# First part of the probabilities' transposes at the beginning of an attention step

## The chip, the cores and the metric

One core of one Trainium2 chip runs the whole program; the weights and activations are in its HBM at the start and the result is written there. The metric is the device time in microseconds (us). Three runs of the kernel before gave 1155.04, 1155.28 and 1155.72 us, median 1155.28. Matrix products and transposes run on TensorE (PE), elementwise work and reductions on VectorE (DVE), activations and copies on ScalarE (ACT), some elementwise work on GpSimd (POOL). SyncE (SP) issues most transfers. Each engine works through its own queue in order and waits there for what it needs from the others.

## The reference

A decoder of two layers on a sequence of 512 tokens with a width of 1024. Layer 1 is a retention layer. Its result gives keys and values once for layer 2, which is a sparse attention: 16 heads in 4 groups, each head with a compressed branch, a branch over selected blocks and a window branch. The change lies in layer 2. For 512 tokens the 8 blocks of 64 all fit into the selection of 16, and the window is 512 long, so the second and third branch are plain causal attentions over all keys, with keys and values of their own:

```
s = einsum('bgrqd,bgkd->bgrqk', q, k) * scale
p = softmax(where(valid, s, NEG), axis=-1)
o = einsum('bgrqk,bgkd->bgrqd', p, v)
out = gates[..., 0:1] * o_c + gates[..., 1:2] * o_s + gates[..., 2:3] * o_w
y = (silu(gate) * out) @ w_out
h = h + y
```

A gated per-layer embedding and an RMS norm end each layer and the network.

## The kernel before

Every matrix product in fp32 is made of three products of rounded parts (`mm3`, line 349: high by high, high by low, low by high). So each operand has a high part, written by an ACT copy, and a low part, written by a DVE subtraction; `split_psum` (line 363) does both from an accumulator bank. All accumulators are PSUM banks of 128 x 512, by tag (line 272): "d" 2 banks for dense work, "s" 3 for scores, "pt" 2 for transposes, "o" 1 for a head's result. A tag's banks are taken in turn, and a bank is taken again when all who read it are done.

The order of the instructions on every engine is the order in which the program issues them; nothing is scheduled anew. Weights come as a stream of blocks of 512 KB: `W.tick(2)` (line 146) issues, twice, the low part of one weight block on DVE (line 205), the high part of another on ACT (line 190) and the gain of a third on POOL (line 176); each low part also lets SP issue the next block's transfer.

Layer 2 is a loop over 4 groups (`g`) of 8 steps (`u`, line 1036). A step belongs to head `u // 2` and branch `u % 2`: branch 0 is the selected one, whose keys also hold the 32 compressed keys, branch 1 the window. In step `u` the kernel does these things, in the order of lines 1045 to 1077:

- `scores` of the next step (line 912): the products of queries and keys into three "s" banks, then on DVE the causal mask (lines 942, 945), the maximum of each row (947) and the compressed scores (951), and on ACT the exponentials with their sums (954). The products have 15 matmuls in odd steps, whose next branch has compressed keys, and 12 in even ones.
- `fill(0)`, `fill(1)`, `fill(2)`: pieces of dense work, each 12 matmuls on PE. They come in a fixed order by `between` (line 34) and `PLAN` (line 1032): halves of a gate projection (evacuated by line 752 on ACT and 753 on DVE), halves of a query projection (739 and 740), pairs of tiles of the output projection of a pair of heads (1015 on DVE, one "d" bank for each tile). A step has one to four of them.
- `scale_probs` of the next step (line 960): the reciprocal of the sums and the gate on DVE (963, 964), then four scalings of the probabilities in place on POOL (967).
- `probs_T(u, 0)` (line 969): two "pt" banks of four transposes of the step's own probabilities (line 976), each followed by its `split_psum` into the operands `tH` and `tL`.
- `probs_T(u, 1)`: the two transposes that are left, into one more bank ("pt", or "d" where no dense piece stands before it), and its split.
- `W.tick(2)`, the rest of the compressed branch's softmax, and in even steps `cmp_T` (line 902): four transposes of the compressed probabilities into a "pt" bank (line 906), which ACT (909) and DVE (910) evacuate.
- `values` (line 981): the products of the transposed probabilities with the values into "o", in odd steps followed by the head's gating and split (993 to 995).

`probs_T` and `values` share the single pair `tH`, `tL`. The probabilities have two buffers. Step 7 of a group projects the next group's keys before anything else; after it the next group's values are projected through "d" and "pt" banks in turn (line 1083), each with a split. In the very first step `fill(0)` stands ahead of the scores.

Of the kernel before, what the change touches and what calls it, by code (L numbers as in the profile page):

```python
# [33 lines left out]
def between(g, h):  # L34

    def out(g, pair):
        return [("nout", g, 2 * pair), ("nout", g, 2 * pair + 1)]

    if g == 3:
        return ([("gate", 3, 0)] + out(2, 1), [("gate", 3, 1), ("gate", 3, 2)], out(3, 0),  # L40
                [("gate", 3, 3), ("emb", 1, 0), ("emb", 1, 1)])[h]
    q = [("q", g + 1, h - 1), ("q", g + 1, h)]
    if g == 0 and h < 2:
        return q if h else [("gate", 0, 0), ("gate", 0, 1)]
    return [("gate", g, h)] + (q if h % 2 else out(g - (h == 0), int(h == 0)))
# [191 lines left out]
def decoder(ctx: ExitStack, tc: tile.TileContext, x, xT, stream, cst, msk, gains, fnorm, out):  # L237
# [34 lines left out]
    def psum(tag, shape=None):  # L272
        n = {"d": 2, "s": 3, "pt": 2, "o": 1}[tag]
        return ps.tile([128, 512], F32, name=tag, bufs=n)
# [88 lines left out]
    def split_psum(h, l, src):  # L363
        act.activation(h, src, AF.Copy)  # L364
        dve.tensor_sub(l, src, h.bitcast(F32))  # L365
# [21 lines left out]
    for k in range(NK):  # L387
        g = gn[:, G_RET + k:G_RET + k + 1]
# [85 lines left out]
    def run(g):  # L474
        for _ in g:
            pass
# [235 lines left out]
    def v_proj(g, t, p, bank="d", tick=True, o=None):  # L712
        if o is None:
            o = psum(bank)[:, :256]
            v_sums(t, o, p, 0)
        else:
            v_sums(t, o, p[2:], 6)
        split_psum(v2H[:, t], v2L[:, t], o[:, :256])
        if g == 0:
            act.activation(bg[:, t], o[:, 256:], AF.Tanh, scale=0.5)  # L720
        if tick:
            W.tick()
        if t == 3:
            for q in p:
                q.done()

    def v_pieces(g):
        if g == 0:
            return [W.get("kvb", r, min(384, 1024 - r), 0, 304) for r in (0, 384, 768)]
        return [W.get("kvv", 512 * a, 512, 256 * g, 256) for a in (0, 1)]  # L730
# [27 lines left out]
    def k_proj(g, b):  # L758
        p = W.get("kv", 0, 1024, 1024 + 512 * b + 128 * g, 128)
        o = psum("d")  # L760
        wst(p, o)
        if b == 0:
            m = slice(32 * g, 32 * g + 32)
            pool.tensor_copy(k2H[0][:, :32], kcH[:, m].bitcast(F32))
            pool.tensor_copy(k2L[0][:, :32], kcL[:, m].bitcast(F32))
        e = 0 if b else 32
        split_psum(k2H[b][:, e:], k2L[b][:, e:], o)
        W.tick()
        p.done()
# [132 lines left out]
    def cmp_T(h):  # L902

        p = psum("pt")
        for i in range(NT):
            pe.transpose(p[:96, 128 * i:128 * i + 128], pc4[h % 2][:, i].rearrange("p r n -> p (r n)"),
                         ident)
        d = pcat[h % 2]
        act.activation(d[:96], p[:96], AF.Copy)
        dve.tensor_sub(d[64:96], p[64:96], d[64:96].bitcast(F32))  # L910
# [49 lines left out]
    def scale_probs(g, u, sm_):  # L960
        h, b = divmod(u, 2)
        Pu = P[u % 2]
        dve.reciprocal(sm_, sm_)
        dve.tensor_mul(sm_, sm_, bg[:, :, 12 * g + 3 * h + b + 1])
        for i in (3, 2, 0, 1):
            w = Pu[:, PO[i]:PO[i] + 128 * i + 128]
            pool.tensor_scalar(w, w, sm_[:, i:i + 1], 1.0, op0=OP.mult, op1=OP.mult)  # L967

    def probs_T(u, part, tag="pt"):
        Pu = P[u % 2]  # L970
        for j0, bank in (((0, (0,)), (1, (1, 3))), ((2, (2,)),))[part]:
            p = psum(tag)
            f = 0
            for j in bank:
                for i in range(j, NT):
                    pe.transpose(p[:, f:f + 128], Pu[:, PO[i] + 128 * j:PO[i] + 128 * j + 128], ident)  # L976
                    f += 128
            c = slice(TO[j0], TO[j0] + f)
            split_psum(tH[:, c], tL[:, c], p[:, :f])

    def values(g, u, o):
        h, b = divmod(u, 2)
        if b:
            pe.matmul(o, vcat[:96, 128 * g:128 * g + 128], pcat[h % 2][:96], start=False, stop=False)
        for j in (0, 1, 3, 2):
            n = 512 - 128 * j
            c = slice(TO[j], TO[j] + n)
            d = slice(128 * b, 128 * b + 128)
            mm3(o[:, 128 * j:], [(v2H[:, j, d], v2L[:, j, d], tH[:, c], tL[:, c])], u % 2 == j == 0,
                b == 1 and j == 2)  # L990
        if b:
            y = g2[h % 2]
            dve.scalar_tensor_tensor(y, o, 0.5, y, op0=OP.mult, op1=OP.mult)
            act.activation(y2H[:, h % 2], y, AF.Copy)
            dve.tensor_sub(y2L[:, h % 2], y, y2H[:, h % 2].bitcast(F32))
# [21 lines left out]
    def fillers(g):  # L1017
        for kind, *i in (b for h in range(4) for b in between(g, h)):
            yield from {"gate": g_proj, "q": q_proj, "nout": pair_tiles, "emb": emb_tiles}[kind](*i)
# [14 lines left out]
    for g in range(GROUPS):  # L1034
        f = fillers(g)
        for u in range(8):
            h = u // 2
            last = (g, u) == (3, 7)
            W.auto = False
            left = 2 * len(between(g, h))  # L1040
            first = 4 if h == 3 else left // 2
            n = PLAN[u] if g == 3 else left - first if u % 2 else first
            steps = [1, 1, 0] if last else PARTS[n]

            def fill(i):
                for _ in range(steps[i]):
                    next(f)

            sums = None
            if u < 7:  # L1050
                nxt = g, u + 1
            elif g < 3:
                k_proj(g + 1, 0)
                k_proj(g + 1, 1)
                nxt = g + 1, 0
            else:
                nxt = None
            if g == u == 0:
                fill(0)
            if nxt:  # L1060
                sums, chain = scores(*nxt)
            if g or u:
                fill(0)
            if sums is not None:
                scale_probs(*nxt, sums)
            probs_T(u, 0)
            next(chain, 0)
            fill(1)
            probs_T(u, 1, "pt" if steps[1] else "d")
            W.tick(0 if last else 2)  # L1070
            next(chain, 0)
            if u % 2 == 0:
                cmp_T(h)
            fill(2)
            if u % 2 == 0:
                o_head = psum("o")
            values(g, u, o_head)
            W.auto = True
        run(f)
        if g < 3:  # L1080
            p = v_pieces(g + 1)
            for t in range(NT):
                v_proj(g + 1, t, p, ("d", "pt")[t % 2], t % 2)
# [101 lines left out]
```

## Time and profile before

The profiled execution took 1155.31 us; its span on the core, from the first instruction's start to the last one's end, is 1153.3 us.

| what | value |
|---|---|
| median of 3 runs | 1155.28 us |
| profiled execution, its span | 1155.31 us, 1153.3 us |
| PE busy | 1132.1 us (98%) |
| DVE busy | 710.4 us (62%) |
| ACT busy | 486.7 us (42%) |
| POOL busy | 317.4 us (28%) |
| loop over the steps | 597.7 to 1081 us |

A row of a timeline gives the start of one instruction or of several merged ones, the time from the first one's start to the last one's end, the engine, the line, what is written and read, and how many were merged (x12). In brackets stands how long the engine sat idle before it, and what ended that. A wait for several things is put down to the one that came last by the profile. Matmuls are pipelined, so on PE the time from one row's start to the next row's start says what a row costs.

### The profile page before, as it was taken

The numbers are of one execution on the slowest core, as the hardware profiler recorded it, in microseconds if no ns is written. First come the engines' busy times: TensorE is split into PE (matmuls) and PEld (weight loads), VectorE is DVE, ScalarE is ACT, GpSimd is POOL, SyncE is SP. The second block draws the span as 40 slices with busy tenths as digits, with TensorE's granted clock in tenths as the row PEclk, the third lists the DMA queues.
The fourth block names the chain that finished last, engine by engine and source line by source line (L and its number), as shares of the span: only waits on it lengthen the run. The fifth ranks groups of instructions, "written<-read, shape, count | busy, mean of one in ns | idle before, by whom it ended". The sixth has DMA issues, their size and how long they took to land. (4 is left out here: it accounts for less than half of the span.)

```text
span 1153.3 us, 15259 instructions
## 1 busy us (share of the span) xinstructions
PE 1132.1 (98%) x5812; PEld 964.3 (84%) x5812; DVE 710.4 (62%) x1226; ACT 486.7 (42%) x916; POOL 317.4 (28%) x357
## 2 busy tenths in 40 slices
PE   9999999999999999999899999999999999999997
PEld 7888888888888888988777889888898888988886
DVE  4746435544634665656577865778468774788555
ACT  6433223223323454545455433444345443444653
POOL 0212003002200212346645332354153431421012
PEclk9999999999999999999999999999999999999999
DMA  8422331222232123244531211222031211221211
GB/s 329 149 97 73 110 101 55 92 101 74 86 116 73 55 78 106 73 152 160 163 110 56 74 37 39 78 85 66 27 93 55 74 56 44 85 85 44 74 37 73
DMA packets 29593, 101.90 MB, mean 88 GB/s; under 512 B 3536, under 2 KB 3792, under 8 KB 29520
## 3 DMA queue, kind: packets, MB, share of 16 engines
q1 hardware_dynamic: 29088, 100.15, 26.8%
q8 instruction: 45, 0.74, 0.3%
q10 hardware_dynamic: 432, 0.79, 0.2%
q14 instruction: 28, 0.23, 0.1%
HBM read 98.83 MB, written 2.10 MB: 88 GB/s over the span
## 5 line engine op out<-in xcount | busy, mean ns | idle before, releaser
L355 PE MATMUL d<-arenaR 128*128 128x512 f32 (+2 forms) x2904 | 676.5, 386 | 2.4 <-ACT arenaR L136 1.0
L355 PEld LDWEIGHTS d<-arenaR 128*128 128x128 f32 x2904 | 524.5, 188 | 103.2 <-DVE arenaF L753 1.4
L355 PE MATMUL s<-arenaR 128*128 128x512 f32 (+8 forms) x1182 | 239.8, 354 | 0.7 <-ACT arenaR L364 0.5
L205 DVE TENSOR_TENSOR arenaR<-arenaF,arenaR 128x1024 fp32r<-128x1024 f32 (+1 forms) x142 | 191.7, 1369 | 70.5 <-ACT arenaR L190 70.3
L355 PEld LDWEIGHTS s<-arenaR 128*128 128x128 f32 x1182 | 200.3, 188 | 30.6 <-ACT arenaR L364 0.7
L190 ACT ACTIVATE arenaR<-arenaF 128x1024 fp32r<-128x1024 f32 (+1 forms) x142 | 145.8, 1048 | 105.6 <-PE s L355 68.4
L176 POOL TENSOR_TENSOR arenaF<-arenaF 128x512 f32<-128x512 f32 x108 | 135.3, 1276 | 99.2 <-DMA arenaF<-stream_dram 94.7
L355 PE MATMUL o<-arenaR 128*128 128x512 f32 (+3 forms) x744 | 128.8, 322 | 6.3 <-DVE arenaR L792 4.1
L967 POOL TENSOR_SCALAR arenaF<-arenaF 128x512 f32<-128x512 f32 (+3 forms) x128 | 67.2, 545 | 232.3 <-ACT arenaR L364 118.8
L355 PEld LDWEIGHTS o<-arenaR 128*128 128x128 f32 x744 | 114.3, 189 | 19.6 <-DVE arenaR L792 5.1
L954 ACT ACTIVATE arenaF<-s,arenaF 128x512 f32<-128x512 f32 (+3 forms) x128 | 67.1, 526 | 101.4 <-DVE arenaF L947 90.6
L365 DVE TENSOR_TENSOR arenaR<-pt,arenaR 128x512 fp32r<-128x512 f32 (+1 forms) x141 | 82.9, 618 | 36.9 <-ACT arenaR L364 34.3
L364 ACT ACTIVATE arenaR<-pt 128x512 fp32r<-128x512 f32 (+1 forms) x141 | 70.8, 541 | 73.3 <-PE pt L976 35.2
L371 POOL TENSOR_TENSOR arenaF<-arenaF 128x1 f32<-128x1 f32 (+1 forms) x25 | 14.2, 570 | 295.3 <-DVE arenaF L370 295.3
L355 PE MATMUL pt<-arenaR 128*128 128x512 f32 (+1 forms) x384 | 75.9, 349 | 0.0
L355 PEld LDWEIGHTS pt<-arenaR 128*128 128x128 f32 x384 | 62.7, 188 | 9.4
L209 DVE SCALAR_TENSOR_TENSOR arenaR<-arenaF,arenaR 128x512 fp32r<-128x512 f32 x64 | 45.7, 763 | 35.1 <-PE pt L355 21.4
L194 ACT ACTIVATE arenaR<-arenaF 128x512 fp32r<-128x512 f32 x64 | 43.1, 720 | 46.7 <-issue 22.3
L947 DVE TENSOR_REDUCE arenaF<-s 128x1 f32<-128x512 f32 (+3 forms) x128 | 59.9, 489 | 3.3
L1015 DVE TENSOR_TENSOR arenaF<-arenaF,d 128x512 f32<-128x512 f32 x64 | 42.4, 683 | 8.6 <-PE d L355 7.8
L976 PEld LDWEIGHTS pt<-arenaF 128*128 128x128 f32 x318 | 38.3, 141 | 10.7 <-DVE arenaR L365 3.1
L976 PE MATMUL pt<-arenaF 128*128 128x128 f32 x318 | 45.1, 273 | 1.9 <-DVE arenaR L365 1.9
(126 smaller groups left out, 704.8 us busy)
## 6 DMA issues: line engine op xcount, KB each, us to landing
arenaF<-stream_dram SPq DMA_DIRECT2D x174, 512.0 KB, 3.6
arenaF<-xT_dram SPq DMA_DIRECT2D x8, 256.0 KB, 5.3
arenaF<-x_dram SPq DMA_DIRECT2D x4, 512.0 KB, 8.4
out_dram<-arenaF SPq DMA_DIRECT2D x3, 512.0 KB, 2.6
arenaF<-cst_dram SPq DMA_DIRECT2D x4, 256.0 KB, 3.9
arenaF<-stream_dram ACTq DMA_DIRECT2D x2, 256.0 KB, 4.2
arenaF<-stream_dram SPq DMA_DIRECT2D x2, 256.0 KB, 5.9
arenaF<-cst_dram SPq DMA_DIRECT2D x1, 512.0 KB, 9.5
```

The source lines that it names most:

```text
L176: self.nc.gpsimd.tensor_mul(r3[:, k], r3[:, k], g[:, k, None].to_broadcast([128, m // 2, w]))
L190: self.nc.scalar.activation(hi[:, :m * w], raw, AF.Copy)
L194: self.nc.scalar.activation(hi[:, c], raw[:, c], AF.Copy, scale=g[:, k:k + 1])
L205: self.nc.vector.tensor_sub(lo[:, :m * w], raw, hi[:, :m * w])
L209: self.nc.vector.scalar_tensor_tensor(lo[:, c], raw[:, c], g[:, k:k + 1], hi[:, c], op0=OP.mult, op1=OP.subtract)
L355: pe.matmul(o, a, b, start=start and i == 0, stop=stop and i == n - 1)
L364: act.activation(h, src, AF.Copy)
L365: dve.tensor_sub(l, src, h.bitcast(F32))
L947: dve.reduce_max(mx[:, i:i + 1], o[:, f:f + 128 * i + 128], axis=mybir.AxisListType.X, negate=True)
L954: act.activation(Pu[:, PO[i]:PO[i] + n], o[:, f:f + n], AF.Exp, bias=mx[:, i:i + 1], accum_out=sm_[:, i:i + 1])
L967: pool.tensor_scalar(w, w, sm_[:, i:i + 1], 1.0, op0=OP.mult, op1=OP.mult)
L976: pe.transpose(p[:, f:f + 128], Pu[:, PO[i] + 128 * j:PO[i] + 128 * j + 128], ident)
```

## The change

The first part of a step's own transposes is issued at the beginning of the step, ahead of the next step's scores. Before, it stood behind the first dense piece and the scaling of the next probabilities. In the very first step, too, the first dense piece now comes behind the scores.

```diff
             else:
                 nxt = None
-            if g == u == 0:
-                fill(0)
+            probs_T(u, 0)
             if nxt:
                 sums, chain = scores(*nxt)
-            if g or u:
-                fill(0)
+            fill(0)
             if sums is not None:
                 scale_probs(*nxt, sums)
-            probs_T(u, 0)
             next(chain, 0)
             fill(1)
             probs_T(u, 1, "pt" if steps[1] else "d")
```

## Rows read from the trace of the kernel before

**Rows 1.** Busy time in the loop over the steps; PE, PEld, DVE, ACT, POOL, clock, DMA.

```profile
597.70:1081.00 483.30, 478.94 (x2668) 415.67 (x2668) 342.83 (x705) 217.32 (x499) 170.39 (x216) 1.00 0.20 63
```

**Rows 2.** Waits of PE in the loop: us in total, times, longest.

```profile
PE pt L976 <- DVE arenaR L365: 1.9, 3, 1.1
...
PE d L355 <- DVE arenaF L753: 0.9, 1, 0.9
...
PE pt L906 <- POOL arenaF L967: 0.9, 4, 0.3
```

**Rows 3.** Timeline of PE in step 1.1: start us, us, what.

```profile
736.39 2.49 PE L355 MATMUL s<-arenaR 128*128 128x512 f32 x15
...
741.49 1.03 PE L976 MATMUL pt<-arenaF 128*128 128x128 f32 x8
...
742.28 3.00 PE L355 MATMUL d<-arenaR 128*128 128x512 f32 x12
```

**Rows 4.** Timeline of DVE in step 1.1.

```profile
737.28 0.30 DVE L945 TENSOR_TENSOR s<-s,masks 128x128 f32<-128x128 f32 x1 [0.51 <-PE s L355]
...
740.93 1.46 DVE L1015 TENSOR_TENSOR arenaF<-arenaF,d 128x512 f32<-128x512 f32 x2
...
742.82 1.29 DVE L365 TENSOR_TENSOR arenaR<-pt,arenaR 128x512 fp32r<-128x512 f32 x2
```

**Rows 5.** Timeline of PE in steps 0.0 to 0.3.

```profile
609.51 2.49 PE L355 MATMUL s<-arenaR 128*128 128x512 f32 x15
...
630.13 0.44 PE L976 MATMUL pt<-arenaF 128*128 128x128 f32 x2 [1.06 <-DVE arenaR L365]
...
630.82 0.61 PE L906 MATMUL pt<-arenaF 128*96 128x128 f32 x4 [0.25 <-POOL arenaF L967]
...
633.20 2.50 PE L355 MATMUL s<-arenaR 128*128 128x512 f32 x15
```

**Rows 6.** Timeline of DVE in steps 0.0 to 0.3.

```profile
609.94 0.69 DVE L910 TENSOR_TENSOR arenaR<-pt,arenaR 32x512 fp32r<-32x512 f32 x1
...
629.39 1.29 DVE L365 TENSOR_TENSOR arenaR<-pt,arenaR 128x512 fp32r<-128x512 f32 x2
...
635.64 0.69 DVE L910 TENSOR_TENSOR arenaR<-pt,arenaR 32x512 fp32r<-32x512 f32 x1
```

**Rows 7.** Timeline of PE in group 3, the beginnings of steps 3.3, 3.4, 3.5, 3.7.

```profile
1025.85 2.50 PE L355 MATMUL s<-arenaR 128*128 128x512 f32 x15
...
1035.32 2.08 PE L355 MATMUL s<-arenaR 128*128 128x512 f32 x12
...
1047.41 2.49 PE L355 MATMUL s<-arenaR 128*128 128x512 f32 x15
...
1072.15 2.91 PE L355 MATMUL d<-arenaR 128*128 128x512 f32 x12
```

**Rows 8.** Timeline of DVE in group 3, line 910.

```profile
1027.43 0.69 DVE L910 TENSOR_TENSOR arenaR<-pt,arenaR 32x512 fp32r<-32x512 f32 x1
...
1047.95 0.69 DVE L910 TENSOR_TENSOR arenaR<-pt,arenaR 32x512 fp32r<-32x512 f32 x1
...
1073.33 0.69 DVE L910 TENSOR_TENSOR arenaR<-pt,arenaR 32x512 fp32r<-32x512 f32 x1 [0.47 <-ACT arenaR L909]
```

**Rows 9.** Timeline of POOL in step 3.3.

```profile
1032.87 3.03 POOL L967 TENSOR_SCALAR arenaF<-arenaF 128x512 f32<-128x512 f32 x4 [9.08 <-ACT arenaR L364]
```

**Rows 10.** Timeline of PE, beginning of step 1.0.

```profile
722.79 2.10 PE L355 MATMUL s<-arenaR 128*128 128x512 f32 x12
```

**Rows 11.** Timeline of DVE, beginning of step 1.0.

```profile
723.41 0.42 DVE L365 TENSOR_TENSOR arenaR<-pt,arenaR 128x256 fp32r<-128x256 f32 x1 [1.51 <-ACT arenaR L364]
```

**Rows 12.** Busy time by stretch ahead of the loop, columns as in the first group.

```profile
568.00:572.00 4.00, 2.01 (x12) 1.30 (x11) 1.40 (x2) 1.58 (x2) 4.00 (x4) 1.00 0.46 176
...
572.00:576.00 4.00, 4.00 (x16) 3.32 (x15) 1.34 (x1) 1.50 (x3) 4.00 (x4) 0.58 0.33 114
```

**Rows 13.** Timeline of PE ahead of the loop.

```profile
572.77 4.43 PE L355 MATMUL d<-arenaR 128*128 128x512 f32 x12
```

## The prediction

> **What bounds the kernel now.** I read the idle time of TensorE (PE) first, then PE's waits, then the timelines of a few steps engine by engine. A step is named g.u here: step 1.5 is u = 5 in group 1; "odd" and "even" go by u. T0 is the part of the probabilities' transposes that the change moves (`probs_T(u, 0)`, two banks of four transposes, "first half" and "second half"), T1 the other part.
>
> The loop over the steps takes 483.3 us of the span, and PE is busy for 478.9 of them at the full granted clock, 1.00, the higher of its two levels [rows 1]. So PE is the bound, and its idle 4.4 us is all that any order of the same instructions can give back there. The table of PE's waits says where these lie [rows 2]: 1.9 us are three waits of T1 for VectorE (DVE) to empty a transpose bank that T0 filled, 0.9 us four waits of the same sort ahead of the compressed branch's transposes (put down to POOL's line 967, but ending when DVE has emptied T0's second bank, see below), 0.9 us one wait for the gate's evacuation, and the rest, 0.7 us, small waits. Everything but the gate's wait, some 3.4 us, goes away if T0 is emptied earlier. Against it stands whatever the early place makes PE wait for. A measurement of this kernel can tell about 0.2% from no change, that is 2.3 us.
>
> **What the change does, part by part.** Nothing is added or removed: T0's 8 transposes on PE, 2 copies on ScalarE (ACT) and 2 subtractions on DVE move from behind the first dense piece to the beginning of the step. T0 issues no DMA and no POOL instruction, and it is not moved past a weight's refresh, so the queues of SP and POOL keep their order. On ACT its copies go ahead of the exponentials, which wait for DVE's maxima in any case. In step 0.0 the scores, too, now come ahead of the first dense piece; I count that as nothing, since PE has the same work there without a gap.
>
> On PE the move by itself costs nothing: T0 takes 0.79 us (741.49 to 742.28) wherever it stands [rows 3]. Three things around it do not stay as they are.
>
> *First, DVE's queue.* DVE works in order, and the subtractions now stand ahead of the masks and maxima of the next scores. In step 1.1 T0 began on PE at 741.49 and DVE's second subtraction ended at 742.82 + 1.29 = 744.11, so 2.62 us later [rows 3, 4]. If T0 begins with the step at 736.39, DVE is free for the scores 2.6 us into the step; it began them 0.9 us in (737.28). All that follows on DVE in that step is 1.7 us later. Who feels it? In step 1.1 the two dense pieces next to T0 are both output-projection tiles, and each tile takes one of two accumulator banks. The first tile's evacuation began at 740.93, lasted half of the pair's 1.46 us, and so ended at about 741.6, 0.7 us before PE came back for that bank at 742.28 (the third tile). PE comes back at 742.28 in the new order too, since T0, scores and first piece have only changed places. The evacuation now ends at 741.6 + 1.7 = 743.3: a new wait of 1.0 us. By `between` and `PLAN` there are seven such steps (0.5, 1.1, 1.5, 2.1, 2.5, 3.1, 3.5): **+7.0 us**. In other steps the piece is half a gate or query projection, which keeps one bank over two pieces, and 1.7 us on DVE are covered: behind T0's old place there are 1.3 us of subtractions that are no longer there, so the later work of the step (weights' refresh, line 205) starts about when it did.
>
> *Second, the transposes' banks.* There are two, used in turn. Step 0.2 shows it: T1 started at 630.13, once the first of T0's two subtractions (629.39 and 1.29 us for both) was through, and the compressed transposes at 630.82, after the second [rows 5, 6]. So in the odd step that follows, T0's second half takes the bank of the compressed transposes, and that is empty when DVE has done line 910, which stands behind the refresh of two weights. Before, 5 us lay between; now 0.4 us, half of T0. Where a third dense piece precedes the values, line 910 ends in time (about 0.1 us to either side of it in the closest cases, counted as nothing). Where there is none, in steps 0.0, 0.2, 3.2, 3.4 and 3.6, it does not.
> Step 0.1: its scores began at 609.51; less the 0.5 us of waits that step 0.0 loses, T0's second half could start at 609.4, but line 910 ended at 609.94 + 0.69 = 610.6 [rows 5, 6]. Net position 0.7 us late.
> Step 0.3: line 910 ended at 635.64 + 0.69 = 636.3; with the 0.7 us, 637.0. The scores can start 0.4 us later, at 637.4; in the old order with T0 in front it would be 633.20 + 0.8 = 634.0. Net **+3.4 us** up to here, the gains of steps 0.0 and 0.2 (1.8 us) already taken off. A shorter wait of T0's first half, for POOL's scaling behind DVE's longer chain, hides inside it. Step 0.4 then gives back its share of the waits in [rows 2]: **-0.8 us**.
> Group 3: into step 3.3, line 910 ends at 1028.1 and the second half could start at 1025.85 + 0.4 = 1026.25: +1.9. Into 3.5, 1048.65 against 1047.8: +0.85. Into 3.7, 1074.0 against 1072.55: +1.45 [rows 7, 8]. Step 3.3 loses its old 0.6 us of waits. Its scaling of the probabilities ran on POOL from 1032.87 to 1035.9 [rows 9], and the next step began at 1035.3 [rows 7]: T0 of step 3.4 needs it at once, and with DVE's chain 1.9 us and PE about 1.3 us later I put +0.8. In step 3.4 the gate's wait of 0.9 us [rows 2] grows by 0.6 (the chain's 1.3 us, less the lateness PE has by then). Together **+5.0 us**.
> The wait for this bank is no row of before. Its bounds are 0 (the bank is free after all) and the end of line 910; I take the latter, since the banks are taken in turn and waited for [rows 5, 6]. Below nothing is excluded beyond the gains counted.
> After the value projection of groups 1 to 3 the same holds for its last tile: its evacuation ended at 723.41 + 0.42 = 723.85, PE wants the bank at 722.79 + 0.4 = 723.2 [rows 10, 11]: 0.65, say 0.7 with the wake-up; **+2.1 us**.
>
> *Third, the clock.* From 568 to 572 us PE was busy 2.0 of 4.0 us, and from 572 to 576 its granted clock averaged 0.58, much of it at the lower level; 12 matmuls took 4.43 us there against 3.00 at the full clock [rows 3, 12, 13], a loss of some 1.5 us. Around step 0.3 over 3 us of five are waits, which leaves PE idler than that; around the other waits it is busier. I count one such fall, **+1.5 us**; the bounds are none and one at each of the four longest waits, 0 and 6 us.
> The Trainium skill (TensorE: Matmul & The Clock Gate, "Why this matters for your kernels") warns of an idle gap between bursts of matmuls, after which the engine is back at half its clock. The row goes further than the rule: PE fell there while it was still busy half of the time, with matmuls between its waits. By the rule one long gap costs something here, as in the sum; by the row the shorter waits may too, which is the last of the rivals.
>
> **Sum.** 3.4 - 0.8 + 7.0 + 5.0 + 2.1 + 1.5 = 18.2 us. The profiled execution took 1155.31 us, span 1153.3 and 2.0 around it, and the median of the runs is 1155.28, so 1155.3 + 18.2 = **1173.5 us**.
>
> **The rivals.**
> *The early split pays (faster).* The 3.4 us of waits go and nothing takes their place: 1155.3 - 3.4 = 1151.9 us. For it: T0 is emptied 5 us earlier, which is what those waits lacked. It decides if DVE's chain moves by less than the 0.7 us that the first tile's bank has in hand in step 1.1, and line 910 is through within 0.4 us of a step's start. The rows give 1.7 us, and line 910 over 2 us late. 4%.
> *Gains and waits cancel.* DVE and PE both have to be less late than the rows say, or the two orders come to the same because other work hides both: about 1155.3 us. 5%.
> *Only one kind of wait comes.* Say the dense tiles' evacuation keeps ahead, because the scores' chain is shorter than it looks: 18.2 - 7.0, 1166.5 us; or the banks of the transposes are free and only the 7.0 us come, less 2.6 of gains: about 1160 us. 13%.
> *The clock falls at each long wait.* Three more falls of 1.5 us: 1178 us. For it: each is a wait of 1.2 to 2 us, and PE's 2 us of idleness were enough from 568 to 572 us [rows 12]. Against: they are shorter than that sum, and each stands between stretches without a gap. 8%.
>
> **How the numbers follow.** The forecast has 70%, its own range 1166 to 1179 (the clock's bounds, and 0.7 to 1.2 us for each of seven waits). The range of 8 in 10 reaches down into the third rival and up past the fourth: 1162 to 1181. Slower by over 0.2%: 70 + 13 + 8 = 91%; within 0.2%: 5%; faster: 4%.
>
> **What would show it.** In PE's waits after the change: about seven of 1 us ahead of a dense tile for line 1015; waits of T0 for DVE's line 910 at the start of steps 0.1, 0.3, 3.3, 3.5 and 3.7, the longest in 0.3, and for line 365 at steps 1.0, 2.0 and 3.0; the 1.9 us of T1 gone; a granted clock under 1.00 only near step 0.3. In odd steps DVE's first mask starts 2.6 us after the step's start. I am wrong if the evacuation in step 1.1 still ends before PE returns, or if T0's second half starts without a wait while line 910 is still to come.

## The result, and the profile after the change

The changed kernel takes 1173.48 us (median of 4 runs, 1173.15 to 1173.90) beside 1155.16 us for the kernel before (4 runs): ratio 1.0158, interval 1.0140 to 1.0176. The prediction was 1173.5. The profiled execution took 1173.67 us, its span is 1171.9. The sum came out; several of its terms did not, and that is what the rest is about.

The page's busy times and the loop (columns as in [rows 1]; the loop is 18.6 us longer, so the window is):

```profile
PE 1137.4 (97%) x5812; PEld 968.5 (83%) x5812; DVE 711.2 (61%) x1226; ACT 487.2 (42%) x916; POOL 320.6 (27%) x357
```

```profile
597.70:1099.60 501.90, 484.76 (x2671) 420.11 (x2671) 343.97 (x705) 217.87 (x499) 173.77 (x216) 0.99 0.19 60
```

The instructions are the same in number. PE's idle time in the loop went from 4.4 to 17.1 us, and its busy time from 478.9 to 484.8, partly because the granted clock is no longer 1.00 throughout. Where the idle time lies is in the table of PE's waits (engine, what it writes, its line, whom it waited for: us in total, times, longest), which answers to [rows 2]:

```profile
PE d L355 <- DVE arenaF L1015: 5.4, 7, 0.8
PE pt L976 <- DVE arenaR L910: 5.4, 5, 1.7
PE pt L976 <- POOL arenaF L967: 2.7, 2, 2.2
PE pt L976 <- DVE arenaR L365: 1.5, 3, 0.5
PE d L355 <- DVE arenaF L753: 1.3, 1, 1.3
```

The first three lines are new; the three waits for line 365 are no longer T1's but lie behind the value projections; the gate's wait for line 753 grew from 0.9. The old waits of T1 and of the compressed transposes are gone. The seven waits for line 1015 look like this in step 1.1, which answers to [rows 3] (first PE, then DVE):

```profile
741.06 1.04 PE L976 MATMUL pt<-arenaF 128*128 128x128 f32 x8
741.85 2.58 PE L355 MATMUL s<-arenaR 128*128 128x512 f32 x15
744.27 2.91 PE L355 MATMUL d<-arenaR 128*128 128x512 f32 x12
747.96 3.02 PE L355 MATMUL d<-arenaR 128*128 128x512 f32 x12 [0.79 <-DVE arenaF L1015]
```

```profile
742.38 1.29 DVE L365 TENSOR_TENSOR arenaR<-pt,arenaR 128x512 fp32r<-128x512 f32 x2 [0.39 <-ACT arenaR L364]
743.59 0.29 DVE L945 TENSOR_TENSOR s<-s,masks 128x128 f32<-128x128 f32 x1
...
747.23 1.28 DVE L1015 TENSOR_TENSOR arenaF<-arenaF,d 128x512 f32<-128x512 f32 x2
```

DVE's first mask stands 2.53 us behind T0 (743.59 - 741.06), where it stood 0.9 us behind the step's start [rows 4]. The pair of evacuations ends at 748.51, its first half about 0.64 earlier, and PE, which is through with the first piece at 747.2, sits until 747.96. The bracket shows 0.79 us of idleness. From the start of one step to the next the loss is larger, 14.90 us against 13.87, so 1.03: the matmuls' modelled tails reach into the wait.

Step 0.3 is the dearest place. PE, POOL and DVE around its start (compare [rows 5, 6]):

```profile
632.85 0.50 PE L355 MATMUL o<-arenaR 128*128 128x256 f32 x2 [0.40 <-DVE arenaR L365]
635.54 1.44 PE L976 MATMUL pt<-arenaF 128*128 128x128 f32 x8 [2.19 <-POOL arenaF L967]
636.73 4.16 PE L355 MATMUL s<-arenaR 128*128 128x512 f32 x15
640.73 2.44 PE L355 MATMUL d<-arenaR 128*128 128x512 f32 x10
```

```profile
631.87 4.07 POOL L967 TENSOR_SCALAR arenaF<-arenaF 128x512 f32<-128x512 f32 x4 [2.80 <-ACT arenaR L739]
```

```profile
632.72 2.61 DVE L205 TENSOR_TENSOR arenaR<-arenaF,arenaR 128x1024 fp32r<-128x1024 f32 x2
635.36 0.69 DVE L910 TENSOR_TENSOR arenaR<-pt,arenaR 32x512 fp32r<-32x512 f32 x1
```

And the same work in the kernel before, POOL and DVE:

```profile
629.48 2.06 POOL L967 TENSOR_SCALAR arenaF<-arenaF 128x512 f32<-128x512 f32 x4 [1.60 <-ACT arenaR L364]
631.50 3.02 POOL L176 TENSOR_TENSOR arenaF<-arenaF 128x512 f32<-128x512 f32 x2
```

```profile
631.52 4.08 DVE L205 TENSOR_TENSOR arenaR<-arenaF,arenaR 128x1024 fp32r<-128x1024 f32 x2
```

T0 waited for its data, not for a bank. The four scalings on POOL took 4.07 us where they had taken 2.06, because DVE's refresh of the weights (line 205) now runs beside them. Before, they were done when it began, and it ran beside POOL's line 176 instead and took 4.08 us; now it took 2.61. Line 910 was through at 636.05, before it could matter. And the scores took 4.0 us from start to start (636.73 to 640.73) instead of the 2.4 of step 1.1 (741.85 to 744.27). Their granted clock (windows, columns as in [rows 1]; the clock is the third number from the end):

```profile
636.00:638.00 2.00, 2.00 (x11) 1.76 (x12) 0.78 (x3) 1.09 (x2) 1.94 (x2) 0.79 0.81 303
638.00:640.00 2.00, 2.00 (x9) 1.95 (x9) 1.89 (x5) 0.48 (x1) 0.00 (x0) 0.50 0.37 147
...
1040.00:1043.00 3.00, 3.00 (x12) 2.67 (x10) 1.94 (x4) 0.60 (x1) 0.00 (x0) 0.50 0.68 273
```

The clock fell to its lower level twice, here behind the 2.2 us wait and in step 3.3 behind a wait of 1.71 us. The beginnings of steps 3.3 and 3.4 on PE, against [rows 7]:

```profile
1037.43 0.60 PE L976 MATMUL pt<-arenaF 128*128 128x128 f32 x4
1039.74 0.97 PE L976 MATMUL pt<-arenaF 128*128 128x128 f32 x4 [1.71 <-DVE arenaR L910]
1040.36 3.95 PE L355 MATMUL s<-arenaR 128*128 128x512 f32 x15
...
1049.92 1.44 PE L976 MATMUL pt<-arenaF 128*128 128x128 f32 x8 [0.50 <-POOL arenaF L967]
```

Here the wait is the one that was forecast: the first half of T0 runs, the second stands until line 910 has emptied the bank.

### The profile page after: what moved, and what is told of

It is laid out like the page before. It is cut to its first block, busy times and chain, and to the rows that moved or that the text cites. A ratio compares the mean times of both kernels' runs of the same rounds, so it can differ in the third digit from the quotient of the medians.

```text
span 1171.9 us, 15262 instructions
## 1 busy us (share of the span) xinstructions
PE 1137.4 (97%) x5812; PEld 968.5 (83%) x5812; DVE 711.2 (61%) x1226; ACT 487.2 (42%) x916; POOL 320.6 (27%) x357
## 5 line engine op out<-in xcount | busy, mean ns | idle before, releaser
L355 PE MATMUL d<-arenaR 128*128 128x512 f32 (+2 forms) x2904 | 669.3, 384 | 8.3 <-DVE arenaF L1015 5.6
L355 PE MATMUL s<-arenaR 128*128 128x512 f32 (+8 forms) x1182 | 245.2, 359 | 0.7 <-ACT arenaR L364 0.5
L176 POOL TENSOR_TENSOR arenaF<-arenaF 128x512 f32<-128x512 f32 x108 | 139.1, 1309 | 91.3 <-DMA arenaF<-stream_dram 91.3
L967 POOL TENSOR_SCALAR arenaF<-arenaF 128x512 f32<-128x512 f32 (+3 forms) x128 | 69.7, 564 | 257.4 <-DVE arenaF L964 223.2
L976 PE MATMUL pt<-arenaF 128*128 128x128 f32 x318 | 47.7, 276 | 9.8 <-DVE arenaR L910 5.4
```

The costliest lines, as they stand in the source:

```text
L176: self.nc.gpsimd.tensor_mul(r3[:, k], r3[:, k], g[:, k, None].to_broadcast([128, m // 2, w]))
L355: pe.matmul(o, a, b, start=start and i == 0, stop=stop and i == n - 1)
```

## The experiments

Each kernel was compared with runs of the kernel before on the same chip, whose median was 1154.86, 1155.15 and 1156.58 us in the three groups of runs (kernels 1 to 4; kernels 5 to 8; kernel 10 and the second run of the changed kernel). Single runs spread more there than in the first comparison, by up to 0.3% to either side, so medians and ratios are read together.

**Which of the two queues costs what.** The first two kernels each take one of the two suspected places in DVE's queue away. Kernel 1 puts the compressed transposes and their evacuation (line 910) ahead of the weights' refresh:

```diff
             probs_T(u, 1, "pt" if steps[1] else "d")
-            W.tick(0 if last else 2)
-            next(chain, 0)
             if u % 2 == 0:
                 cmp_T(h)
+            W.tick(0 if last else 2)
+            next(chain, 0)
             fill(2)
```

> The changed kernel with one more edit: in even steps the compressed transposes and their evacuation are issued ahead of the refresh of two weights, not behind it. Theory (the second half of the early transposes waits for the compressed branch's bank, which line 910 empties too late because it stands behind the refresh): PE's five waits for line 910 (5.4 us in its table, 6.4 us by the distance from one start to the next) go, and so does the second fall of the clock (1.4 us, at step 3.3), so 1173.5 - 7.7 = 1165.8 us; the seven waits for line 1015 and the two for POOL's line 967 stay. Rival (the banks are not the cause, the early transposes are in the way of other work wherever they stand): 1173 us, with the waits put down to something else.

Measured: 1167.33 us, ratio 1.0112 (1.0097 to 1.0127). Its waits of PE:

```profile
PE d L355 <- DVE arenaF L1015: 5.7, 7, 0.8
PE pt L976 <- POOL arenaF L967: 1.9, 2, 1.7
PE pt L976 <- DVE arenaR L365: 1.5, 3, 0.5
```

Every wait for line 910 is gone and those for line 1015 stay, which is the theory. In step 0.3 the scalings now take 2.05 us again and the wait for them is 0.16 us, since line 205 stands behind line 910 and starts (633.74) when POOL has nearly done them (634.11). But POOL's wait in step 3.4 grew from 0.50 to 1.73 us, as PE no longer comes late to it: a wait had hidden another. The time came out 1.5 us above the expected 1165.8. One fall of the clock was expected to be left and this profile has two in the loop: one at step 0.3, and one behind the 1.73 us in step 3.4, whose scores took 3.29 us from start to start where 2.0 us is usual.

Kernel 2 keeps the changed order on PE but splits T0's banks where T0 was split before (`probs_T0` issues the transposes of `probs_T(u, 0)` alone and returns the banks):

```diff
-            probs_T(u, 0)
+            t0 = probs_T0(u)
...
                 scale_probs(*nxt, sums)
+            for c, p in t0:
+                split_psum(tH[:, c], tL[:, c], p)
             next(chain, 0)
```

> The changed kernel with the early transposes kept at the beginning of the step on PE, but their copies on ACT and subtractions on DVE issued at their old place, behind the scaling. Theory (the seven waits for line 1015 come from DVE's two subtractions ahead of the scores' masks): those seven waits go, 6.9 us; the first mask of an odd step starts 0.9 us after the scores' start again; the old waits of the later transposes (1.9 + 0.9 us) come back; the waits for line 910 stay and the clock still falls at steps 0.3 and 3.3. Sum about 1169 us, 1167 to 1171. Rival (it is PE's order, not DVE's, that makes the dense tiles wait): 1173 us or more, with the waits for line 1015 still there.

Measured: 1168.27 us, ratio 1.0110 (1.0093 to 1.0127). L988 is the line of T0's transposes in this kernel:

```profile
PE pt L988 <- DVE arenaR L910: 7.8, 5, 2.6
PE pt L976 <- DVE arenaR L365: 1.5, 2, 1.2
PE pt L988 <- DVE arenaR L365: 1.5, 3, 0.5
```

The counterpart: no wait for line 1015 is left and the five for line 910 stay, longer now, and T1 waits for T0's split as it did before the change. The clock fell once in this loop, in step 0.3, not twice as expected. So the two kinds are separate, and both are places in DVE's queue.

**Which steps.** Kernel 3 has T0 early in odd steps alone, kernel 4 in even steps alone (`u % 2 == 0`):

```diff
-            probs_T(u, 0)
+            early = u % 2 == 1
+            if early:
+                probs_T(u, 0)
...
                 scale_probs(*nxt, sums)
+            if not early:
+                probs_T(u, 0)
```

> The early place in odd steps alone, the old place in even ones. Theory (all of the large losses lie in odd steps: seven waits for line 1015, five for line 910; even steps hold the gains and the three waits behind the value projection): 1173 us, between 1170 and 1175, as slow as the whole change. Rival (the loss is spread over the steps, as a cost of each moved transpose): half of the 18.3 us, 1164 us.

> The early place in even steps alone, the old place in odd ones. Theory: the gains of even steps (2.8 us, three waits of the later and four of the compressed transposes) against three waits of 0.7 us behind the value projection, about 0.6 us for the scaling ahead of step 3.4 and 0.4 us more for the gate there: 1155.2 + 0.3, 1154.5 to 1156.5 us, with no wait for line 910 or line 1015 and no fall of the clock in the loop. Rival (loss spread over the steps): 1164 us.

Measured: odd steps 1171.07 us, ratio 1.0137 (1.0122 to 1.0152); even steps 1155.38 us, ratio 1.0008 (0.9998 to 1.0017). The largest waits of the odd kernel:

```profile
PE pt L976 <- DVE arenaR L910: 5.7, 5, 1.7
PE d L355 <- DVE arenaF L1015: 5.1, 7, 0.8
```

and the two largest of the even one:

```profile
PE d L355 <- DVE arenaF L753: 1.6, 1, 1.6
PE pt L976 <- DVE arenaR L365: 1.5, 3, 0.5
```

The odd steps carry the loss. In them T0 meets the bank of the even step's compressed transposes at the step's start, and the seven waits for line 1015 lie there too, where the two dense pieces behind the scores are both output tiles. The even steps gain their old waits and lose as much behind the value projections and at the gate.

**Both cures, and the value projection.** Kernel 5 joins the edits of kernels 1 and 2.

> Both cures at once: the compressed transposes and their evacuation ahead of the weights' refresh, and T0's split at its old place. Theory: the waits for line 1015 (6.9 us) and for line 910 (5.4 us) go together, since each was a position in DVE's queue and nothing else. What is left against the kernel before is 2.1 us behind the value projections, about 1 us for POOL's scaling in step 3.4 and one or two clock falls of 1.5 us, less up to 2.8 us of old waits that are still gained: 1158 us, 1155 to 1161. Rival: the late split makes line 910's place worth nothing, or something other than DVE's queue holds T0's banks; then the waits for line 910 of the late-split kernel (7.8 us) stay and the time is 1164 or more.

Measured: 1158.71 us, ratio 1.0037 (1.0022 to 1.0052). Its largest waits:

```profile
PE pt L976 <- DVE arenaR L365: 2.0, 2, 1.2
PE pt L988 <- DVE arenaR L365: 1.5, 3, 0.5
```

Neither line 1015 nor line 910 appears any more. The first line is T1 waiting for the late split of T0, the old wait come back; the second lies behind the value projections. Kernel 8 takes that one out of the changed kernel by its banks:

```diff
-                v_proj(g + 1, t, p, ("d", "pt")[t % 2], t % 2)
+                v_proj(g + 1, t, p, ("pt", "d")[t % 2], t % 2)
```

> The changed kernel with the banks of the value projection's tiles taken the other way round (transposes' bank, dense, transposes', dense), so that the last tile stands in a dense bank. Theory: the waits of steps 1.0, 2.0 and 3.0 (0.69, 0.68 and 0.68 us) are for the last tile's bank, which T0's second half takes; they go and nothing else changes: 1173.5 - 2.05 = 1171.4 us, 1171 to 1172. Rival: T0 waits there for the operands' buffers or for DVE's queue, whichever bank the tile stands in: 1173.5 us.

Measured: 1169.33 us, ratio 1.0123 (1.0107 to 1.0139). The three waits for line 365 are gone, those for lines 1015, 910 and 967 remain (5.4, 4.7 and 3.4 us), so the three were for the last tile's bank. But against 1173.48 the gain is 4.2 us instead of 2.05; its profile has no fall of the clock in the loop, and those had been some 3 us. Kernel 10 puts this edit into kernel 5.

> The kernel with both cures (compressed transposes ahead of the refresh, T0's split at its old place), and the value projection's banks swapped as well. Theory: the three waits behind the value projections are 1.5 us by the table of waits and about 2 us with the wake-ups, and go: 1158.7 - 2.0 = 1156.7 us, 1156 to 1157.5. What is left against the kernel before is the new wait of T1 for the late split of T0 in group 0 (2.0 us). Rival: with T0's split late, its second half needs the other transposes' bank too and the wait only moves to the next reader: 1158.7 us.

Measured: 1156.78 us, ratio 1.0005 (0.9994 to 1.0016); T1's 2.0 us are its largest wait, and the three behind the value projections are gone. With these three mended the early place costs nothing that can be measured, and with a late split it gains nothing either.

**A version that beats both.** Kernel 6 takes the early place only where it had something to gain and nothing to lose (the rest of the edit as in kernel 3):

```diff
+            early = g == 0 and u in (0, 2, 4)
```

> T0 at the beginning of the step in steps 0.0, 0.2 and 0.4 alone, at its old place in all others. Theory: the early place pays where a step's own compressed transposes and T1 waited for T0's banks, which was in group 0's even steps, 2.8 us in all; no odd step moves, so no evacuation is late, and no even step behind a value projection moves. So 1155.2 - 2.8 = 1152.4 us, 1151.8 to 1153.5. Rival: the gain is lost again at the next step, where the scores or the scaling set PE's start, and it is 1155 us like the kernel with all even steps.

Measured: 1152.43 us (12 runs, 1150.92 to 1153.72), ratio 0.9976 (0.9966 to 0.9986). Its waits:

```profile
PE d L355 <- DVE arenaF L753: 1.1, 2, 1.0
PE o L355 <- DVE arenaR L365: 0.5, 2, 0.3
PE o L355 <- ACT arenaR L364: 0.4, 1, 0.4
PE d L355 <- DVE arenaF L1015: 0.3, 1, 0.3
```

No transpose waits any more. The waits of [rows 2] that belong to T1 and the compressed transposes were 2.8 us, and 2.7 came. One of the seven, 0.2 us in step 1.2, lies in a step that this kernel leaves alone; it is gone too, and why was not looked into.

**The clock.** Kernel 7 leaves T0 at its old place in the two steps where the clock fell:

```diff
+            early = (g, u) not in ((0, 3), (3, 3))
```

> The changed kernel with T0 at its old place in two steps, 0.3 and 3.3, which had the two longest waits (2.19 and 1.71 us) and both falls of the clock (1.67 and 1.36 us). Theory: the falls hang on those waits, so all four terms go: 1173.5 - 6.9 = 1166.6 us, 1165.5 to 1168, with a granted clock of 1.00 through the loop. Rival: the clock falls in group 0 and 3 for the stretches' general idleness and not for these two waits; then only 3.9 us go, 1169.6 us, and the clock is under 1.00 somewhere near.

Measured: 1166.82 us (1165.28 to 1167.94), ratio 1.0101 (1.0084 to 1.0118), with a granted clock of 1.00 throughout its loop. That is the theory's number. But this profile lacks the fall ahead of the loop too, which every other profile here has, and kernel 8 does not allow the theory. Its step 0.3 is the changed kernel's, 0.08 us later:

```profile
631.95 4.07 POOL L967 TENSOR_SCALAR arenaF<-arenaF 128x512 f32<-128x512 f32 x4 [2.79 <-ACT arenaR L739]
```

```profile
635.62 1.44 PE L976 MATMUL pt<-arenaF 128*128 128x128 f32 x8 [2.18 <-POOL arenaF L967]
636.81 2.56 PE L355 MATMUL s<-arenaR 128*128 128x512 f32 x15
```

```profile
636.00:638.00 2.00, 1.93 (x13) 1.80 (x14) 0.78 (x3) 1.09 (x2) 2.00 (x3) 1.00 0.85 332
638.00:640.00 2.00, 2.00 (x15) 1.87 (x14) 1.93 (x6) 0.40 (x1) 0.02 (x1) 1.00 0.40 147
```

The same wait, the same engines beside it, and the scores run at the full clock; the 1.71 us wait of step 3.3 is there too, without a fall. So the changed kernel ran once more, unedited.

> The changed kernel once more, nothing edited, for the clock alone: the kernel with the swapped banks had the same two waits (2.18 us in step 0.3, 1.71 us in 3.3) at the same place of the loop, without a fall of the clock. Theory: whether the clock falls at such a wait differs from execution to execution, so this profile may have two falls, one or none in the loop, and the times spread between 1170.5 (none) and 1173.9 (two). Rival: the falls belong to this kernel and this place: both come again, at the scores of steps 0.3 and 3.3, and the median is 1173.5 us within 0.4.

Measured: 1171.15 us (1168.59 to 1172.53), ratio 1.0127 (1.0105 to 1.0148). The windows of steps 0.3 and 3.3:

```profile
636.00:638.00 2.00, 1.88 (x9) 1.69 (x9) 0.51 (x1) 0.55 (x1) 2.00 (x3) 0.55 0.75 277
638.00:640.00 2.00, 2.00 (x7) 1.70 (x7) 1.72 (x4) 0.65 (x2) 0.41 (x1) 0.60 0.58 211
1038.00:1040.00 2.00, 1.00 (x7) 0.92 (x8) 1.61 (x3) 0.28 (x2) 0.00 (x0) 1.00 0.83 260
1040.00:1042.00 2.00, 2.00 (x15) 1.94 (x14) 1.58 (x4) 0.35 (x1) 0.00 (x0) 1.00 0.63 256
```

One fall this time, in step 0.3, none in 3.3, behind the same two waits (2.18 and 1.71 us). Nor does a fall need so long a wait: kernel 1 had one at the scores of step 0.3 (3.4 us from start to start), where PE had only waited 0.90, 0.40 and 0.16 us in the 3 us ahead of it. All falls in the loop lie behind waits of PE, but neither their length nor their place decides. What does was not found. Against this second run kernel 8 gains 1.8 us by the medians, close to its theory, and 0.5 us by the ratios; their intervals, 0.2% to either side, are too wide to tell. This also says how far the result is to be trusted: between 1.3 and 1.6% slower. An estimated 1.6 to 3.2 us of it come from how often the clock happened to fall (one or two falls in the profiles, 1.6 us each by the rows of the next section); the mean granted clock of the runs, 0.993 to 0.995 the first time and 0.995 to 0.996 the second, points the same way.

## Why the prediction was right, and where it was not

The direction and the size were right, and for the main reason given: DVE and the accumulator banks are taken in order, and T0's early place puts its split ahead of the scores and its second half onto a bank that is not yet empty. By terms, each measured as PE's lateness against the kernel before, from the start of a step to the start of the next (the two falls of the clock are taken out of step 0.3 and group 3 and have a row of their own):

| term | predicted | measured |
|---|---|---|
| steps 0.0 to 0.3 | +3.4 | +2.3 |
| step 0.4 | -0.8 | -1.3 |
| seven odd steps, line 1015 | +7.0 | +6.9 |
| group 3 | +5.0 | +4.6 |
| behind the value projections | +2.1 | +2.05 |
| clock | +1.5 | +3.2 |
| step 1.2, step 2.3 | 0 | -0.4, +0.9 |
| sum | 18.2 | 18.2 |

*The odd steps* were right to a tenth: 2.53 us until DVE's first mask against 2.6 worked out, and 1.03 us lost in step 1.1 against 1.0. Kernel 2 shows the cause, since the split's place alone takes the seven waits away.

*Step 0.3* was right in place and wrong in mechanism. The step that failed is "A shorter wait of T0's first half, for POOL's scaling behind DVE's longer chain, hides inside it": it was the longer one. The prediction let every instruction keep its duration. But the refresh of the weights now met the scalings instead of line 176: line 205 took 1.5 us less, line 967 2.0 us more. So line 910 was ready 1 us before the forecast and the probabilities later. Kernel 1 confirms it: with line 205 behind, the scalings took 2.05 us. Part of the difference from +3.4 lies earlier: step 0.0 took 10.89 us where it had taken 11.81, a gain of 0.9 where 0.5 was counted.

*Step 2.3* was among the "closest cases, counted as nothing". It waited 0.70 us for line 910 behind a refresh that took 4.09 us beside line 176, where it had taken 3.23: the same effect. In the second run of the changed kernel that wait is not there (four waits for line 910, not five), so "nothing" was within what an execution can show. That the first profile has five waits for line 910, the number forecast, is a coincidence: step 2.3 stands in for step 0.3.

*The clock* was sized for one fall; the first profile had two, the second one. Each cost 1.6 us: from the transposes ahead of the scores to the next dense piece PE took 5.19 us in step 0.3 and 4.40 in step 3.3, and 3.59 and 2.83 in the same places of kernel 8, where the clock stayed up. The row that stood for the fall, 4.43 us for 12 matmuls [rows 13], gave its price well. That the number of falls is a matter of the execution was not in the prediction, whose fourth rival made it a matter of the wait's length: none of the waits of 0.7 to 1.7 us for line 910 had one in the second run. Of the Trainium skill's rule on idle gaps (TensorE: Matmul & The Clock Gate, "Why this matters for your kernels") these runs show the half that a gap can cost the clock; the same gap of 2.18 us also passed without cost, in kernel 8.

So the sum is nearer than its parts, and that it agrees to the tenth is luck: steps 0.0 to 0.4 and step 1.2 together came out 2.0 us lower, group 3 another 0.4, the clock and step 2.3 together 2.6 higher. With one fall, as predicted, and without step 2.3 it would have been about 1171, which is what the changed kernel gave the second time. The rival in which only one kind of wait comes is what kernels 2 and 1 are made to be. Kernel 2, without the waits for line 1015, took 1168.3 us against the rival's 1166.5. Kernel 1, without those for line 910, took 1167.3 against about 1160: the waits behind the value projections, POOL's 1.9 us and the two falls of the clock are left there, which that rival did not count. The rival in which the early split pays is true of three steps: kernel 6.

## What to carry to other kernels

Moving work earlier on the engine that is the bound moves its evacuation ahead in every in-order queue behind it; before asking what the move gains, read how much each bank's evacuation has in hand (here 0.7 us) and what the moved evacuation puts in front of it (1.7 us). A move is not the same in all passes of a loop: the table of waits, read step by step, named three of 32 places with most to gain, and the kernel that moved only those three was the fastest. And when instructions of DVE and POOL come to run beside others than before, their durations are not carried over.

## What was not expected of the hardware

DVE's refresh (line 205, two inputs in SBUF) and POOL's scalings hold each other up. Alone the four scalings take 2.06 us, and in step 1.1 two instructions of line 205 took 2.35; side by side both were done only 4.07 us after the scalings began, with the scalings ending last. POOL's loss fell on one instruction, the third scaling; here it is in step 0.3 and, undisturbed, in step 1.1:

```profile
633.10 2.39 POOL L967 TENSOR_SCALAR arenaF<-arenaF 128x128 f32<-128x128 f32 x1
...
750.22 0.37 POOL L967 TENSOR_SCALAR arenaF<-arenaF 128x128 f32<-128x128 f32 x1
```

It began behind DVE's first instruction (632.72) and ended at 635.49, when DVE's second had ended (635.32); the other three scalings took the time that they take in step 1.1. DVE lost 0.3 us. The Trainium skill names a cause (SBUF — State Buffer, "Who interferes with whom": a VectorE instruction with two inputs in SBUF contends with a GpSimd instruction that reads SBUF, the ports that they share are an exclusive lock, and the order of issue decides who blocks). The trace agrees: 4.07 us is nearly the sum of the two, 4.4, and the scaling that came second was through only when both of DVE's instructions were.

The granted clock fell to its lower level, 1.2 GHz, behind a wait of 2.2 us in two executions and not in a third whose rows in that step are the same. In the first profile the two falls cost 1.6 us each.
